# Transposing five mixer tiles by TensorE into PSUM instead of by 32x32 blocks on VectorE, and a wider spread of the in-place norm scaling

## Chip, core and metric

One core of one Trainium2 chip runs the whole layer. The metric is the device time of one execution in microseconds (us). The engines are called by the profile's names: PE is TensorE, with PEld for its weight loads; DVE is VectorE; ACT is ScalarE; POOL is GpSimd; SP is SyncE, which issues the DMAs.

## What is computed

A hybrid decoder layer on 256 positions of width 2048, all in float32, cut here to what matters:

```
x  = LN0(alpha*x + 0.5*SwiGLU_1(x))              # FFN, hidden width 5504
z  = x @ W_in                                    # columns: conv B, C, h | hgrn q, f, i, g | two gates
yA = B * causal_dwconv3(C * h)
f  = lb + (1-lb)*sigmoid(f);  q = silu(q);  k = 1-f
yB = rmsnorm(chunked_gla(q, k, i, log f)) * norm_w * silu(g)
m  = sigmoid(gate_conv)*(yA @ Wa) + sigmoid(gate_hgrn)*(yB @ Wb)
x  = LN1(alpha*x + m @ W_out)
x  = LN2(alpha*x + 0.5*SwiGLU_2(x))
x  = LN3(alpha*x + sigmoid(x @ W_pg) * (p @ W_pp))
```

LN is a layer norm with a gain row and a bias row; layers, batch and depth are 1.

## The kernel before

**Matmuls.** Every product is a list of units. A unit is 512 output columns over up to 16 row blocks of 128, for both halves of the 256 positions (t = 0 and 1, 128 partitions each). Weights come in pairs of row blocks (512 KB, a "weight pair" below): one DMA on SP's queue into a `raw` buffer (4 of them, line 669), one cast by ACT into a high half `wh` (line 682), one subtraction by DVE into a low half `wl` (line 684, the "split"). Six buffers hold such split pairs, a few more in some stages but none more in the mixer. The left operand is held in the same way as high and low halves, so each row block takes three matmuls on PE: high by high (line 736), high by low weight (737), low by high (738), each 128x512, summed in PSUM. Each weight pair serves six of them for t = 0 and six for t = 1. When a unit's sum is complete, its epilogue reads it from PSUM on ACT or DVE.

**Turning tiles.** A result that is to be the left operand of a later product, or that the recurrence needs with channels on partitions, has to be transposed. There are two ways in the code: `transposed` (line 176) has PE multiply four 128x128 pieces with an identity into a PSUM tile `tp` (2 buffers); `turn_blocks` (line 197) has DVE transpose 32x32 blocks, 16 instructions of 32 partitions x 128 elements for a 128x512 tile. The norms use the first way; the FFN's hidden tiles, most of the merge's tiles m and the mixer's f, q, u, b and y use the second. `halves` (line 182) then makes the high half on ACT (line 189) and the low half on DVE (line 190).

**The mixer** runs twice seven units (f, q, i as `v`, g, C as `cst`, h, B as `b`), two groups of four heads each. `hgrn_units` and `conv_units` give the epilogues. `hgrn` is a generator of some 40 steps: kb, qd and AT on DVE, small float32 matmuls on PE (lines 394, 424, 444, 453 to 456), squares and a square root on ACT, then y (line 467).

**Order.** The code counts ticks, one per weight pair and half t, that is every six large matmuls. `defer(n, fn)` runs `fn` n ticks later, and each tick runs one step of the generator. `affine_rows` (line 241) finishes a norm in place: after a norm, x holds only the centred and scaled value; two DMAs of 256 KB on SP's queue bring 512 columns of gain and bias, spread over all partitions, into one of the four `raw` buffers, and four ticks later DVE multiplies and adds for both t (lines 250, 251). This is done for four column groups c after each of the first three norms. `settle(c)` runs deferred work early when the next product needs these columns. On top of this a scheduler in the build orders each engine's instructions by its own timing model; at run time every engine works in that order.

Of the kernel before, what the change touches and what calls it, by code (L numbers as in the profile page):

```python
# [17 lines left out]
P = 128  # L18
# [47 lines left out]
def hybrid_layer(ctx: ExitStack, tc: tile.TileContext, x, p, ln_g, ln_b, ffn1_w_in, ffn1_w_out, mix_w_in,  # L66
# [189 lines left out]
    def layer_norm(t, i, scale, stat):  # L256

        mean, r = moments(t, scale)

        def operand(c, xc):  # L260
            y = st.tile([P, CC], F32, tag="silu", name="y", bufs=2)
            tp = transposed(xc, 4)
            if t == 0 and c < 2:
                gate["pe"] = state["turned"], 1
            for a in range(4):
                k = i * 16 + 4 * c + a
                nc.scalar.activation(y[:, a * P : (a + 1) * P], tp[:, a * P : (a + 1) * P], AF.Identity,  # L267
                                     bias=gbT[:, 48 + k : 49 + k], scale=gbT[:, k : k + 1])
            halves(stat, t, c, y, 4, "x")

        for c in range(4):
            xc = xt[t][:, c * CC : (c + 1) * CC]
            norm = nc.vector.tensor_scalar(out=xc, in0=xc, scalar1=mean, scalar2=r, op0=ALU.subtract, op1=ALU.mult)
            defer((6 if t == 0 else 4) + c, lambda c=c, xc=xc: operand(c, xc))
            if c == 1 and t == 0:
                gate["lo"] = norm.ins, 2
        if t == NT - 1:
            for c in range(4):
                unsettled.add(c)
                defer(16 + 6 * c, lambda c=c: affine_rows(i, c, range(NT)))  # L280

    def layer_norm_out(t, gb):
        mean, r = moments(t, 1.0)
# [100 lines left out]
    def hgrn(j, ys, qT, fT, kT, v, sg):  # L384
# [63 lines left out]
        for t in range(NT):  # L448
            po = ps_h.tile([P, CC], F32, tag="hg", name="po")
            for h in range(4):  # L450
                c = slice(h * P, (h + 1) * P)
                if t == 0:
                    nc.tensor.matmul(po[:, c], AT[:, h, 0, :], v[0][:, c], start=True, stop=True)
                else:
                    nc.tensor.matmul(po[:, c], A01[:, h, :], v[0][:, c], start=True, stop=False)
                    nc.tensor.matmul(po[:, c], AT[:, h, 1, :], v[1][:, c], start=False, stop=True)
            yield
            ss = st.tile([P, 4], F32, tag="ss", name="ss", bufs=2)
            junk = st.tile([P, P], F32, tag="junk", name="junk", bufs=1)
            for h in range(4):  # L460
                nc.scalar.activation(junk, po[:, h * P : (h + 1) * P], AF.Square, accum_out=ss[:, h : h + 1])
            r = rsqrt_of(ss, 4, 1.0 / P, RMS_EPS)
            yield
            y = st.tile([P, CC], F32, tag="h", name="y", bufs=3)
            for h in range(4):
                c = slice(h * P, (h + 1) * P)
                nc.vector.scalar_tensor_tensor(out=y[:, c], in0=po[:, c], scalar=r[:, h : h + 1], in1=sg[t][:, c],
                                               op0=ALU.mult, op1=ALU.mult)
            yield
            yT = rtile([P, 4, P], F32, tag="qd", name="yT", bufs=2)  # L470
            turn_blocks(yT, y, 4)
            halves(ys, t, j, yT.rearrange("p a b -> p (a b)"), 4, "g")
            yield

    ya, yb = Stat(), Stat()
# [1 line left out]
    def hgrn_units(j):  # L477
# [3 lines left out]
        def epi_f(t, acc):  # L481
# [5 lines left out]

            def fn():
                cols = slice(t * P, (t + 1) * P)
                turn_blocks(hold["f"][:, :, cols], s, 4)  # L490
                for h in range(4):
                    i = 4 * j + h
                    nc.vector.tensor_scalar(out=hold["f"][:, h, cols], in0=hold["f"][:, h, cols],
                                            scalar1=oml[:, i : i + 1], scalar2=lb[:, i : i + 1],
                                            op0=ALU.mult, op1=ALU.add)
                nc.vector.tensor_scalar(out=hold["k"][:, :, cols], in0=hold["f"][:, :, cols], scalar1=-1.0, scalar2=1.0,
                                        op0=ALU.mult, op1=ALU.add)

            defer(2, fn)

        def epi_q(t, acc):
            s = st.tile([P, CC], F32, tag="h", name="s", bufs=3)
            nc.scalar.activation(s, acc, AF.Silu)
            defer(2, lambda: turn_blocks(hold["q"][:, :, t * P : (t + 1) * P], s, 4))

        def epi_v(t, acc):
            v[t] = rtile([P, CC], F32, tag=f"v{t}", name="v")
# [13 lines left out]
    def conv_units(j):  # L521
# [6 lines left out]
        def epi_h(t, acc):  # L528
# [6 lines left out]

            def fn():
                uT, cT = hold["u"], hold["c"]
                turn_blocks(uT[:, :, 2 + t * P : 2 + (t + 1) * P], u, 4)
                for h in range(4):
                    i = 4 * j + h  # L540
                    o = cT[:, h, t * P : (t + 1) * P]
# [4 lines left out]
                                                       scalar=cw[:, 8 * kk + i : 8 * kk + i + 1], in1=o,  # L546
                                                       op0=ALU.mult, op1=ALU.add)

            defer(2, fn)

        def epi_b(t, acc):
            b = st.tile([P, CC], F32, tag="h", name="b", bufs=3)
            nc.scalar.copy(b, acc)  # L553

            def fn():
                z = st.tile([P, CC], F32, tag="h", name="z", bufs=3)
                zv = z.rearrange("p (h c) -> p h c", h=4)
                turn_blocks(zv, b, 4)
                nc.vector.tensor_tensor(out=zv, in0=zv, in1=hold["c"][:, :, t * P : (t + 1) * P], op=ALU.mult)
                halves(ya, t, j, z, 4, "g")  # L560

            defer(2, fn)

        for base, epi in ((CW, epi_c), (2 * CW, epi_h), (0, epi_b)):
            units.append(Unit(x1, wm, 0, 16, base + j * CC, CC, epi))
# [210 lines left out]
```

## Time and profile before

| | us |
|---|---|
| median of 3 runs (2276.3 to 2281.53) | 2278.85 |
| the profiled execution, its own time | 2279.4 |
| its span, first to last instruction | 2277.6 |
| PE busy | 2232.2 |
| DVE busy | 1591.9 |
| ACT busy | 996.6 |

The span runs from the first to the last instruction, and 1.8 us of the time lie around it. Stages by time: first FFN to 715, its norm to 745, the mixer's fourteen units to 1088, the merge to 1445, second FFN to 2165, the last product and norm to the end. PE's busy time counts a matmul until its modelled end, so two matmuls 0.23 us apart overlap; the counts of matmuls in a stretch, multiplied by the pace, tell more than the busy share. In the stretches view, PEclk is the granted clock as a share of 2.4 GHz.

### The profile page before, as it was taken

To read this page: it belongs to the slowest core of one execution; us is meant where nothing else is said; L and a number is where in the kernel's file an instruction comes from. 1 tells how busy PE (TensorE), PEld (TensorE's weight loads), DVE (VectorE), ACT (ScalarE), POOL (GpSimd) and SP (SyncE) were. 2 spreads that over 40 slices of the span, in tenths; PEclk is the share of its full clock that TensorE was granted. 3 is DMA by queue.
4 is the path that set the end of the run, shared out by engine and by line. 5 is a ranking of instruction groups with operands and counts; after the bars stand their busy time and mean duration, and the time that the engine had idled before them with its cause. 6 is when DMAs were issued, how large, how long until landed. Compare 5 with 4: busy or idle time off the path is not lost.

```text
span 2277.6 us, 27257 instructions
## 1 busy us (share of the span) xinstructions
PE 2232.2 (98%) x10074; PEld 1856.1 (81%) x10074; DVE 1591.9 (70%) x2534; ACT 996.6 (44%) x1160; POOL 10.5 (0%) x32
## 2 busy tenths in 40 slices
PE   9999999999999999899999999999999999999997
PEld 7888888888897788688788888788888888889875
DVE  6766566755685979978854975678755767467667
ACT  5443444444345343433444444634433444344463
POOL 1000000000000000000000000000000000000000
PEclk9999999999999999999999999999999999999999
DMA  8565566565563564464566565566565666655574
GB/s 284 185 210 196 185 195 198 181 203 192 159 216 118 178 204 137 165 202 128 175 197 199 175 202 194 168 205 231 192 199 184 200 194 197 199 183 185 164 227 148
DMA packets 225337, 430.01 MB, mean 189 GB/s; under 512 B 13740, under 2 KB 22452, under 8 KB 225204
## 3 DMA queue, kind: packets, MB, share of 16 engines
q1 hardware_dynamic: 225204, 428.27, 58.3%
q8 instruction: 79, 1.29, 0.2%
q14 instruction: 54, 0.44, 0.1%
HBM read 426.12 MB, written 2.10 MB: 188 GB/s over the span
## 4 chain that ended last, share of the span: by engine, by line
PE 82%; DVE 11%; DMA 3%; issue 2%; ACT 1%; SPq 0%; DVEq 0%; ACTq 0%
PE acc L737 27%; PE acc L738 27%; PE acc L736 27%; DVE wl L684 3%; DMA gb<-in_ln_g_dram 1%; PE gp L424 1%; DVE yT L202 1%; DVE uT L202 1%; DVE fT L202 1%; DMA raw<-in_ple_w_gate_dram 1%; DMA raw<-in_ffn_w_in_dram 1%; DMA raw<-in_mix_w_in_dram 1%; DVE z L202 1%; ACT y L267 1%; ACT wh L682 0%
## 5 line engine op out<-in xcount | busy, mean ns | idle before, releaser
L682 ACT CAST wh<-raw 128x1024 fp32r<-128x1024 f32 (+2 forms) x804 | 830.7, 1037 | 1063.2 <-PE acc L738 812.6
L684 DVE TENSOR_TENSOR wl<-raw,wh 128x1024 fp32r<-128x1024 f32 (+2 forms) x804 | 958.6, 1207 | 459.1 <-ACT wh L682 425.8
L737 PE MATMUL acc<-wl,xh 128*128 128x512 f32 (+1 forms) x2240 | 869.5, 389 | 11.1 <-DVE wl L684 11.1
L736 PE MATMUL acc<-wh,xh 128*128 128x512 f32 (+1 forms) x2240 | 867.2, 389 | 9.4 <-ACT wh L682 3.8
L738 PE MATMUL acc<-wh,xl 128*128 128x512 f32 (+1 forms) x2240 | 869.8, 389 | 1.8 <-DVE xl L190 1.8
L737 PEld LDWEIGHTS acc<-wl,xh 128*128 128x128 f32 x2240 | 423.0, 189 | 97.5 <-DVE wl L684 15.5
L736 PEld LDWEIGHTS acc<-wh,xh 128*128 128x128 f32 x2240 | 423.0, 189 | 94.5 <-ACT wh L682 5.7
L738 PEld LDWEIGHTS acc<-wh,xl 128*128 128x128 f32 x2240 | 422.9, 189 | 85.6 <-DVE xl L190 3.5
L736 PE MATMUL acc<-wh,gh 128*128 128x512 f32 x880 | 343.1, 390 | 2.9 <-ACT b L553 2.9
L738 PE MATMUL acc<-wh,gl 128*128 128x512 f32 x880 | 342.8, 390 | 0.0
L737 PE MATMUL acc<-wl,gh 128*128 128x512 f32 x880 | 342.5, 389 | 0.0
L202 DVE STREAM_TRANSPOSE hT<-h 32x128 f32<-32x128 f32 (+1 forms) x704 | 210.8, 300 | 9.8
L736 PEld LDWEIGHTS acc<-wh,gh 128*128 128x128 f32 x880 | 165.4, 188 | 37.5 <-ACT b L553 3.4
L738 PEld LDWEIGHTS acc<-wh,gl 128*128 128x128 f32 x880 | 165.3, 188 | 34.1
L737 PEld LDWEIGHTS acc<-wl,gh 128*128 128x128 f32 x880 | 165.3, 188 | 34.0
L309 DVE TENSOR_TENSOR h<-silu,acc 128x512 f32<-128x512 f32 (+1 forms) x44 | 29.6, 672 | 53.1 <-PE acc L738 53.1
L189 ACT CAST gh<-hT 128x512 fp32r<-128x512 f32 (+1 forms) x48 | 29.4, 613 | 63.3 <-DVE hT L202 63.3
L305 ACT ACTIVATE silu<-acc 128x512 f32<-128x512 f32 (+1 forms) x44 | 25.7, 585 | 51.0 <-PE acc L738 51.0
L322 DVE TENSOR_TENSOR x<-x,acc 128x512 f32<-128x512 f32 x32 | 21.8, 683 | 31.2 <-PE acc L738 31.2
L267 ACT ACTIVATE y<-tp,gbT 128x128 f32<-128x128 f32 x96 | 36.2, 474 | 7.9 <-PE tp L179 4.7
L190 DVE TENSOR_TENSOR gl<-hT,gh 128x512 fp32r<-128x512 f32 (+1 forms) x48 | 32.4, 674 | 0.0
L202 DVE STREAM_TRANSPOSE hT<-m 32x128 f32<-32x128 f32 x96 | 29.1, 303 | 1.4
(142 smaller groups left out, 727.0 us busy)
## 6 DMA issues: line engine op xcount, KB each, us to landing
raw<-in_ffn_w_in_dram SPq DMA_DIRECT2D x320, 512.0 KB, 4.7
raw<-in_mix_w_in_dram SPq DMA_DIRECT2D x176, 512.0 KB, 4.7
raw<-in_ffn_w_out_dram SPq DMA_DIRECT2D x168, 512.0 KB, 5.3
raw<-in_mix_w_out_dram SPq DMA_DIRECT2D x32, 512.0 KB, 5.1
raw<-in_ple_w_gate_dram SPq DMA_DIRECT2D x32, 512.0 KB, 5.5
raw<-in_ffn_w_in_dram SPq DMA_DIRECT2D x32, 384.0 KB, 3.9
raw<-in_branch_w_conv_dram SPq DMA_DIRECT2D x16, 512.0 KB, 5.5
raw<-in_branch_w_hgrn_dram SPq DMA_DIRECT2D x16, 512.0 KB, 4.5
```

The costliest lines, as they stand in the source:

```text
L189: nc.scalar.copy(hf, src)
L190: nc.vector.tensor_tensor(out=lf, in0=src, in1=hf.bitcast(F32), op=ALU.subtract)
L202: nc.vector.transpose(dst[32 * b : 32 * b + 32, :nb, 32 * q : 32 * q + 32], cols[32 * q : 32 * q + 32, :, b, :])
L267: nc.scalar.activation(y[:, a * P : (a + 1) * P], tp[:, a * P : (a + 1) * P], AF.Identity, bias=gbT[:, 48 + k : 49 + k], scale=gbT[:, k : ...
L305: nc.scalar.activation(silu[t][:, :w], acc, AF.Silu)
L309: nc.vector.tensor_tensor(out=h[:, :w], in0=silu[t][:, :w], in1=acc, op=ALU.mult)
L424: nc.tensor.matmul(gp[:, (h * 2 + t) * 64 : (h * 2 + t + 1) * 64], kd[:, h, t * P : (t + 1) * P], qd[:, h, t, :], start=True, stop=True)
L682: nc.scalar.copy(h[:, :n, :w], raw[:, :n, :w])
L684: nc.vector.tensor_tensor(out=l[:, :n, :w], in0=raw[:, :n, :w], in1=h[:, :n, :w].bitcast(F32), op=ALU.subtract)
L736: nc.tensor.matmul(acc, sh, wh[:, a, : u.width], start=first, stop=False)
L737: nc.tensor.matmul(acc, sh, wl[:, a, : u.width], start=False, stop=False)
L738: nc.tensor.matmul(acc, sl, wh[:, a, : u.width], start=False, stop=last)
```

## The change

1. The tiles f, q, u, b and y of the mixer are transposed by PE through `transposed` instead of by `turn_blocks` on DVE. f is scaled by DVE straight out of PSUM; q and u are copied from PSUM by ACT; b is multiplied with the convolution's result straight out of PSUM; y goes through `to_stat`, which takes both halves out of PSUM. Where these steps were deferred by 2 ticks they are deferred by 3, and the generator has one more empty step ahead of y's.
2. The four calls of `affine_rows` after each norm are deferred by 40, 60, 80 and 100 ticks instead of 16, 22, 28 and 34.

```diff
-                defer(16 + 6 * c, lambda c=c: affine_rows(i, c, range(NT)))
+                defer(40 + 20 * c, lambda c=c: affine_rows(i, c, range(NT)))
...
             yield
-            yT = rtile([P, 4, P], F32, tag="qd", name="yT", bufs=2)
-            turn_blocks(yT, y, 4)
-            halves(ys, t, j, yT.rearrange("p a b -> p (a b)"), 4, "g")
+            yield
+            to_stat(ys, t, j, y, 4, "g")
...
-                turn_blocks(hold["f"][:, :, cols], s, 4)
+                tp = transposed(s, 4)
                 for h in range(4):
                     i = 4 * j + h
-                    nc.vector.tensor_scalar(out=hold["f"][:, h, cols], in0=hold["f"][:, h, cols],
+                    nc.vector.tensor_scalar(out=hold["f"][:, h, cols], in0=tp[:, h * P : (h + 1) * P],
...
-            defer(2, lambda: turn_blocks(hold["q"][:, :, t * P : (t + 1) * P], s, 4))
+
+            def fn():
+                tp = transposed(s, 4)
+                nc.scalar.copy(hold["q"][:, :, t * P : (t + 1) * P], tp.rearrange("p (h c) -> p h c", h=4))
+
+            defer(3, fn)
...
-                turn_blocks(uT[:, :, 2 + t * P : 2 + (t + 1) * P], u, 4)
+                tp = transposed(u, 4)
+                nc.scalar.copy(uT[:, :, 2 + t * P : 2 + (t + 1) * P], tp.rearrange("p (h c) -> p h c", h=4))
...
+                tp = transposed(b, 4)
                 z = st.tile([P, CC], F32, tag="h", name="z", bufs=3)
                 zv = z.rearrange("p (h c) -> p h c", h=4)
-                turn_blocks(zv, b, 4)
-                nc.vector.tensor_tensor(out=zv, in0=zv, in1=hold["c"][:, :, t * P : (t + 1) * P], op=ALU.mult)
+                nc.vector.tensor_tensor(out=zv, in0=tp.rearrange("p (h c) -> p h c", h=4), in1=hold["c"][:, :, t * P : (t + 1) * P], op=ALU.mult)
                 halves(ya, t, j, z, 4, "g")
```

**DVE, where the first head group's b and y are turned** (z is b turned, then multiplied; yT is y turned; gl the low half of an operand). Before:

```order
L684 TENSOR_TENSOR wl<-raw,wh 128x1024
L202 STREAM_TRANSPOSE z<-b 32x4x32 x11
L202 STREAM_TRANSPOSE yT<-y 32x4x32 x16
L202 STREAM_TRANSPOSE z<-b 32x4x32 x5
L684 TENSOR_TENSOR wl<-raw,wh 128x1024 x4
L559 TENSOR_TENSOR z<-z,cT 128x512
L190 TENSOR_TENSOR gl<-yT,gh 128x512
L202 STREAM_TRANSPOSE z<-b 32x4x32 x13
```

The same place on DVE in the changed kernel, where the split is line 689 and b's product line 564:

```order
L467 SCALAR_TENSOR_TENSOR y<-po,r,sg 128x128 x4
L689 TENSOR_TENSOR wl<-raw,wh 128x1024 x3
L564 TENSOR_TENSOR z<-tp,cT 128x512
L190 TENSOR_TENSOR gl<-tp,gh 128x512
L689 TENSOR_TENSOR wl<-raw,wh 128x1024
L190 TENSOR_TENSOR gl<-z,gh 128x512
L564 TENSOR_TENSOR z<-tp,cT 128x512
L689 TENSOR_TENSOR wl<-raw,wh 128x1024
```

The 32 transposes that stood in one piece between two splits are gone, and between two splits of this piece stand at most two other instructions.

**PE, in the changed kernel, where y of t = 0 is turned** (po is the recurrence's output, suf and AT its operands; lines 741 to 743 are the three large matmuls). In the row of before only the po matmuls stood here:

```order
L743 MATMUL acc<-wh,xl 128x512
L455 MATMUL po<-v,suf 128x128
L179 MATMUL tp<-ident,y 128x128 x2
L456 MATMUL po<-v,AT 128x128
L455 MATMUL po<-v,suf 128x128
L179 MATMUL tp<-ident,y 128x128 x2
L456 MATMUL po<-v,AT 128x128
```

y's transposes now stand in PE's queue among the po matmuls of t = 1, 30 large matmuls behind the po matmuls of t = 0 from which y comes; the large matmuls follow behind them.

**DVE, in the last product, at its third and fourth column group** (sig is the gate, x_92 and x_93 are x of t = 0 and 1, gb the gain and bias). Before:

```order
L250 TENSOR_TENSOR x_92<-x_92,gb 128x512
L250 TENSOR_TENSOR x_93<-x_93,gb 128x512
L684 TENSOR_TENSOR wl<-raw,wh 128x1024
L634 TENSOR_TENSOR sig<-sig,pp 128x512
L251 TENSOR_TENSOR x_92<-x_92,gb 128x512
L251 TENSOR_TENSOR x_93<-x_93,gb 128x512
L635 SCALAR_TENSOR_TENSOR x_93<-x_93,sig 128x512
L215 BN_STATS bn<-x_93 128x6
L684 TENSOR_TENSOR wl<-raw,wh 128x1024 x4
```

The last rows with gain and bias in the changed kernel (lines 639 and 640 are 634 and 635 of before):

```order
L251 TENSOR_TENSOR x_92<-x_92,gb 128x512
L251 TENSOR_TENSOR x_93<-x_93,gb 128x512
L250 TENSOR_TENSOR x_92<-x_92,gb 128x512
L250 TENSOR_TENSOR x_93<-x_93,gb 128x512
L640 SCALAR_TENSOR_TENSOR x_92<-x_92,sig 128x512
L689 TENSOR_TENSOR wl<-raw,wh 128x1024
L640 SCALAR_TENSOR_TENSOR x_93<-x_93,sig 128x512
L251 TENSOR_TENSOR x_92<-x_92,gb 128x512
L251 TENSOR_TENSOR x_93<-x_93,gb 128x512
L215 BN_STATS bn<-x_92 128x6
L215 BN_STATS bn<-x_93 128x6
L639 TENSOR_TENSOR sig<-sig,pp 128x512
```

Before, nine splits follow the last of these scalings; now the last of all splits stands between the multiplication and the addition of the fourth group. On SP's queue the four pairs of loads move behind 789, 795, 803 and 804 of the 804 weight pairs, from 784, 789, 791 and 795; in the mixer they move behind 293, 302, 313 and 322, from 281, 283, 286 and 290.

## Rows read from the trace of the kernel before

**Rows 1.** The page: the span, then busy time, share of the span and instructions of PE and DVE.

```profile
span 2277.6 us, 27257 instructions
PE 2232.2 (98%) x10074; PEld 1856.1 (81%) x10074; DVE 1591.9 (70%) x2534; ACT 996.6 (44%) x1160; POOL 10.5 (0%) x32
```

**Rows 2.** The stretches view: stretch, its length, busy time and count of each engine, granted clock, DMA share, GB/s. First the first FFN, then the mixer, then pieces of the mixer.

```profile
50.00:600.00 550.00, 550.00 (x2428) 455.61 (x2428) 361.05 (x543) 230.22 (x238) 0.00 (x0) 1.00 0.60 194
745.00:1115.00 370.00, 352.31 (x1668) 292.80 (x1668) 322.42 (x646) 147.81 (x187) 3.81 (x3) 0.98 0.53 166
755.00:815.00 60.00, 53.85 (x231) 42.71 (x230) 52.97 (x98) 21.98 (x24) 0.00 (x0) 0.97 0.64 192
815.00:915.00 100.00, 100.00 (x516) 85.36 (x515) 86.37 (x167) 39.77 (x58) 2.77 (x2) 1.00 0.51 160
915.00:960.00 45.00, 37.34 (x148) 29.44 (x147) 43.72 (x102) 16.85 (x19) 0.00 (x0) 0.92 0.44 147
1095.00:1115.00 20.00, 16.12 (x59) 12.43 (x58) 19.36 (x52) 6.87 (x8) 0.00 (x0) 0.83 0.45 148
```

**Rows 3.** The stretches view of line 736 alone (one of the three large matmuls of a row block): PE and PEld busy time and count, granted clock, DMA share, GB/s.

```profile
50.00:600.00 550.00, 314.99 (x809) 151.79 (x810) 1.00 0.60 194
745.00:1115.00 370.00, 176.59 (x449) 86.08 (x449) 0.98 0.53 166
755.00:815.00 60.00, 28.49 (x73) 14.02 (x73) 0.97 0.64 192
815.00:915.00 100.00, 47.85 (x123) 22.94 (x122) 1.00 0.51 160
```

**Rows 4.** The chain of waits, start and us: a group of 16 small matmuls of the recurrence, and four transposes by PE in the merge (tile m). The last row is of the groups view of the merge: those transposes, count, busy us, mean ns of one, idle time before.

```profile
829.17 1.73 PE gp L424 x16
...
1356.39 0.44 PE tp L179 x4
...
L179 PE MATMUL tp<-ident,m 128*128 128x128 f32 x8 | 1.2, 272 | 0.0
```

**Rows 5.** The waits of PE from 745 to 1115 us: who waited for whom, us in all, times, the longest.

```profile
PE acc L737 <- DVE wl L684: 7.8, 7, 3.0
PE acc L736 <- ACT b L553: 5.9, 2, 3.0
PE acc L736 <- ACT wh L682: 3.8, 2, 2.4
```

**Rows 6.** The timeline of DVE around 945 us (start, us, instruction, count).

```profile
938.72 5.04 DVE L202 STREAM_TRANSPOSE fT<-s 32x128 f32<-32x128 f32 x16
943.79 2.36 DVE L684 TENSOR_TENSOR wl<-raw,wh 128x1024 fp32r<-128x1024 f32 x2
...
951.07 1.90 DVE L202 STREAM_TRANSPOSE fT<-s 32x128 f32<-32x128 f32 x6
953.00 3.50 DVE L684 TENSOR_TENSOR wl<-raw,wh 128x1024 fp32r<-128x1024 f32 x3
```

**Rows 7.** The timeline of PE just behind it; in brackets the idle time before an instruction and what ended it.

```profile
954.28 0.54 PE L737 MATMUL acc<-wl,xh 128*128 128x512 f32 x1 [3.02 <-DVE wl L684]
...
955.05 0.63 PE L736 MATMUL acc<-wh,xh 128*128 128x512 f32 x1
955.47 0.63 PE L737 MATMUL acc<-wl,xh 128*128 128x512 f32 x1
```

**Rows 8.** The stretches view of line 202 alone, the transposes on DVE, in the mixer; then the groups view of one of their five tiles (count, busy us, mean ns of one, idle before).

```profile
745.00:1115.00 370.00, 95.58 (x317) 0.98 0.53 166
...
L202 DVE STREAM_TRANSPOSE yT<-y 32x128 f32<-32x128 f32 x64 | 19.4, 303 | 0.8
```

**Rows 9.** The groups view: an ACT copy of 128x512 out of PSUM, the low half made out of PSUM (first products) and out of SBUF (y in the mixer), and ACT's casts of weights in the mixer with their idle time before.

```profile
L446 ACT COPY suf<-gp 128x512 f32<-128x512 f32 x2 | 1.2, 585 | 7.5 <-DVE u L534 7.5
...
L190 DVE TENSOR_TENSOR xl<-tp,xh 128x512 fp32r<-128x512 f32 x8 | 5.4, 687 | 3.6 <-ACT xh L189 3.6
...
L190 DVE TENSOR_TENSOR gl<-yT,gh 128x512 fp32r<-128x512 f32 x4 | 2.7, 686 | 0.0
...
L682 ACT CAST wh<-raw 128x1024 fp32r<-128x1024 f32 x112 | 117.2, 1049 | 178.6 <-PE acc L738 86.8 <-DMA raw<-in_mix_w_in_dram 53.5 <-DVE wl L684 28.6
```

**Rows 10.** The last product: PE's only wait from 2200 to 2264 us; then DVE's timeline: a scaling that waits for its load, the last split, the start of the last norm for t = 0 and for t = 1; then the page of DMAs: the gain's loads, count, size, us from issue to landing.

```profile
PE acc L737 <- DVE wl L684: 2.1, 2, 1.2
...
2229.00 1.29 DVE L250 TENSOR_TENSOR x<-x,gb 128x512 f32<-128x512 f32 x2 [2.62 <-DMA gb<-in_ln_g_dram]
...
2250.20 1.21 DVE L684 TENSOR_TENSOR wl<-raw,wh 128x1024 fp32r<-128x1024 f32 x1
2256.93 0.69 DVE L634 TENSOR_TENSOR sig<-sig,pp 128x512 f32<-128x512 f32 x1 [5.52 <-ACT sig L633]
...
2265.48 0.68 DVE L634 TENSOR_TENSOR sig<-sig,pp 128x512 f32<-128x512 f32 x1
...
gb<-in_ln_g_dram SPq DMA_DIRECT2D x16, 256.0 KB, 5.3
```

**Rows 11.** The timeline of ACT and DVE on the way to y of t = 0: the first square of the recurrence's output, the table load for the square root, y.

```profile
885.76 0.28 ACT L461 ACTIVATE junk<-po 128x128 f32<-128x128 f32 x1 [0.26 <-PE po L453]
...
891.15 1.28 ACT L224 ACT_TABLE_LOAD   x1
...
901.63 1.12 DVE L467 SCALAR_TENSOR_TENSOR y<-po,r,sg 128x128 f32<-128x128 f32 x4
```

More of the change, by code (lines that the diff above doesn't have):

```diff
@@ L497, in fn @@
                                         op0=ALU.mult, op1=ALU.add)
-            defer(2, fn)
+            defer(3, fn)
         def epi_q(t, acc):
@@ L503, in epi_q @@
             nc.scalar.activation(s, acc, AF.Silu)
-            defer(2, lambda: turn_blocks(hold["q"][:, :, t * P : (t + 1) * P], s, 4))
+            def fn():
+                tp = transposed(s, 4)
+                nc.scalar.copy(hold["q"][:, :, t * P : (t + 1) * P], tp.rearrange("p (h c) -> p h c", h=4))
+            defer(3, fn)
         def epi_v(t, acc):
@@ L547, in fn @@
                                                        op0=ALU.mult, op1=ALU.add)
-            defer(2, fn)
+            defer(3, fn)
         def epi_b(t, acc):
@@ L555, in fn @@
             def fn():
+                tp = transposed(b, 4)
                 z = st.tile([P, CC], F32, tag="h", name="z", bufs=3)
                 zv = z.rearrange("p (h c) -> p h c", h=4)
-                turn_blocks(zv, b, 4)
-                nc.vector.tensor_tensor(out=zv, in0=zv, in1=hold["c"][:, :, t * P : (t + 1) * P], op=ALU.mult)
+                nc.vector.tensor_tensor(out=zv, in0=tp.rearrange("p (h c) -> p h c", h=4), in1=hold["c"][:, :, t * P : (t + 1) * P], op=ALU.mult)
                 halves(ya, t, j, z, 4, "g")
-            defer(2, fn)
+            defer(3, fn)
         for base, epi in ((CW, epi_c), (2 * CW, epi_h), (0, epi_b)):
```

## The prediction

> **What bounds the kernel now.** I read the page first, then the stretches, then PE's waits, and last the timelines at each wait. PE is busy for 98% of the span [rows 1], so time can be won only where PE loses some. The stretches show where. In the first FFN PE is busy without a break for 550 us at full clock. Line 736 runs 809 times there, so 3 x 809 = 2427 large matmuls take 550 us, 0.2266 us each [rows 2, 3]. That is the pace of a PE that nothing holds up. The mixer falls behind it: 449 x 3 = 1347 large matmuls make 305.2 us, the other 1668 - 1347 = 321 at 1.73 / 16 = 0.108 us make 34.7 us, and the stretch is 370 us long, so 30 us are lost [rows 2 to 4].
>
> The loss is not spread out. From 815 to 915 us the same sum is 369 x 0.2266 + 147 x 0.108 = 99.5 of 100 us: nothing is lost, though DVE is 86% busy and the whole recurrence of the first group runs there. From 755 to 815 it is 219 x 0.2266 + 12 x 0.108 = 50.9 of 60, so 9.1 us are lost; from 915 to 960, 148 x 0.2266 = 33.5 of 45, 11.5 lost; from 1095 to 1115, 59 x 0.2266 = 13.4 of 20, 6.6 lost [rows 2, 3]. Together these three pieces lose **27.2 us**.
>
> They are the pieces in which f, q, b and y are turned. PE's waits in the mixer name only a split by DVE, a cast by ACT, or the copy of b by ACT that makes room in PSUM [rows 5]. The timeline shows why: 16 transposes hold DVE for 5.04 us, then two splits, then 14 more with what belongs to them, and only at 953.00 the split for which PE has waited 3.02 us [rows 6, 7]. The casts and the copy of b are late for the same reason, since ACT's casts stand behind DVE's splits for 28.6 us of the mixer [rows 9]. After such a wait PE runs at half its clock for a while: the next large matmuls start 0.42 us apart instead of 0.23, and the granted clock of the three pieces is 0.97, 0.92 and 0.83 [rows 2, 7]. The 27.2 us contain both the wait and the slow matmuls behind it.
>
> **The change part by part.** *Transposes off DVE.* The mixer has 317 recorded, 95.6 us at 0.303 us each [rows 8]; the program has 20 tiles x 16 = 320. Without them DVE is busy for 322.4 - 95.6 = 226.8 us of some 350, 65%, the share that it has in the first FFN (361 of 550, 66%), where PE loses nothing [rows 2]. The pieces of 16 and 32 that stand ahead of splits are gone from DVE's order. What is late next is the recurrence's chain and the norm's scaling, and the stretch from 815 to 915 shows that the chain alone costs nothing. I take the whole 27.2 us as won, and as a bound that half of it stays (13.6), should the scaling and the recurrence be enough to hold up a split.
>
> *Transposes onto PE.* 20 tiles x 4 = 80. They are on the path, since PE is the bound. The trace has the same thing in the merge: four of them take 0.44 us of PE's chain between two large matmuls [rows 4]. 20 x 0.44 = **8.8 us** added. At the other end stands the record of one, 0.272 us [rows 4]: if the records did not overlap, 80 x 0.272 = 21.8 us. I take 8.8, since that row is the same instruction with the same neighbours.
>
> *What reads the result.* f's scaling, b's product and y's low half read PSUM instead of SBUF on DVE; the low half takes 0.687 us out of PSUM and 0.686 out of SBUF [rows 9], so I take nothing. q and u cost ACT 8 copies of 0.585 us, 4.7 us [rows 9]. ACT is busy for 148 of 370 us in the mixer [rows 2], and its casts wait for 178.6 us there, half of it for PE to give buffers back [rows 9]; that covers the copies. If the cover failed, 4.7 us would be their cost. The new wait is that ACT and DVE stand still at such a read until PE has come to the transposes; behind it stand casts and splits. In the build's order the transposes of f, q, u and b come 12 to 27 large matmuls, 3 to 6 us, behind the end of their unit, and the splits queued behind them are for weight pairs whose buffers PE gives back only then. I take nothing.
>
> *Deferral by one tick more* moves a step by six large matmuls, 1.4 us; nothing needs these tiles that soon.
>
> *Scaling spread out.* In the mixer and the second FFN the loads and the scaling only move; each is two loads of 256 KB on SP's queue, ahead of a weight pair of 512 KB, and two passes over x per half t on DVE. There the loads then lie about ten weight pairs apart instead of three. In the last product they cannot spread: its units come too soon, so `settle` calls for them early, and each load is issued just before it is needed. A load lands after 5.3 us, and DVE waits 2.62 us at one of these scalings already now; PE loses 2.1 us there [rows 10]. In the changed order the last split stands behind the fourth group's multiplication, and five passes of 0.69 us stand between it and the last norm of t = 0. Before, that split is done at 2251.4 and DVE idles for 5.52 us until the gate comes; t = 1 starts in the very moment in which DVE is free, 2265.48 [rows 10]. So whatever delays DVE by more than the 5.5 us lands on the end. The five passes take 3.4 us; a load ahead of the split makes it wait, 2.6 us by that row. 3.4 + 2.6 - 5.5 = 0.5 us; I take **1 us**, since the loads of the third and the fourth group both have to land ahead of it. Bounds: -2 (PE's present 2.1 us go and the tail is covered) and +4 (the wait is a load's whole 5.3 us, and a little more for the second).
>
> *Sum.* -27.2 + 8.8 + 1 = -17.4 us. The profiled execution took 2279.4 us, so 2262.0; it lies 0.55 above the median of the runs, so the forecast is **2261.5 us**.
>
> **A rule against the change.** What the row shows is above: four transposes in 0.44 us of PE [rows 4]. The Trainium skill, page "VectorE: DVE Perf Modes", section "The three transpose paths", puts a 128x128 transpose at 390 ns on TensorE and 311 ns on VectorE, in bfloat16. By that, 80 x 0.39 = 31.2 us would go onto the bound and the result would be 2284; by the row it is 8.8 and 2261.5. The trace does not agree that a transpose costs PE that much when large matmuls stand on both sides of it. The page "TensorE: Matmul & The Clock Gate", section "Part 4: PE-mode transpose", says that transposes do not count as activity for the clock; in the merge's row the large matmuls behind the four come at 0.23 us again, so here that changes nothing.
>
> **The rivals.**
> *A. The bursts are not what matters.* Half of the loss stays, because the scaling of x (each with its load) and the recurrence still stand ahead of splits. For it: by the order of before, the first norm's scaling falls into the first lost piece. Against it: 815 to 915 us, and the other two pieces, which hold no scaling. 2261.5 + 13.6 = 2275.1.
> *B. PE stands at its own transposes (slower).* PE works in order, so a transpose whose tile is not there yet stops the large matmuls behind it. The place is y of t = 0 and the pair of y of t = 1 and b, in both head groups, four stops. y comes at the end of the longest chain: squares, a table load of 1.28 us, the root, then DVE. Before, it is there 15.9 us after the first square [rows 11], while the order now gives it 30 large matmuls, 6.8 us. Against it: in those 15.9 us DVE did the transposes of u, 10 us by 2 x 5.04, which are gone. A stop like the one from 1095 to 1115 costs 6.6 us with the clock's loss [rows 2]. Between my forecast and no change lie 17.4 us, so it decides from the third stop; with four, 2261.5 + 26.4 = 2287.9.
> *C. Each transpose holds PE for its whole record.* 21.8 instead of 8.8: 2274.5. For it only the record's length; against it the chain's row [rows 4]. The skill's 390 ns, named above, belongs here.
> *D. The end takes it back.* The late scalings cost 4 more and each of the four groups stops PE for 2 us in the last product: 2261.5 + 3 + 8 = 2272.5.
> That the change does not do what it says is excluded by the order: the block transposes of the five tiles are gone and 80 pieces stand on PE.
>
> **How the numbers follow.** Forecast 0.68 (2254 to 2269: the low end is without any cost at the end and with the 2.9 us that the mixer loses outside the three pieces won as well, 2261.5 - 3 - 2.9 = 2255.6, less the spread of the runs; the high end is a quarter of the loss staying). A 0.12, B 0.10, C 0.04, D 0.06. The range is 2254 to 2275: it takes in D, C and most of A, and leaves out B and a part of A. About 0.2%, 4.6 us, is what a measurement of this kernel can tell from no change. Slower by more than that needs B: 0.08. Within it lie a third of A and a mild B: 0.07. Faster: 0.85.
>
> **What would show it.** In the changed profile the mixer should have PE busy without a break as in the first FFN, granted clock 1.00, DVE at about 65%, and be some 18 us shorter; four transposes should take 0.44 us of the chain. B would show as PE waiting at line 179 for DVE or ACT, with the clock falling behind it; A as PE waiting at line 742 for splits; D as DVE waiting for gb behind 2190 us and a later start of the last norm. The forecast is wrong if the lost pieces keep their waits, or if new ones appear at the transposes.

## The result, and the profile after

| | before | after |
|---|---|---|
| median, us | 2277.57 (2275.37 to 2281.53, 4 runs) | 2255.12 (2254.24 to 2255.99, 4 runs) |
| ratio after to before | | 0.9900, interval 0.9882 to 0.9917 |
| profiled execution, its span, us | 2279.4, 2277.6 | 2255.39, 2253.7 |

The change makes the kernel 22.5 us faster; 2261.5 was forecast, and the range of 2254 to 2275 holds the result near its low end. The forecast took the median of 2278.85 as its start; against the 2277.57 measured beside the change, it is -22.5 measured to -17.4 forecast.

Every kernel here runs the same 9600 large matmuls, in an order that differs only in short local exchanges, so both traces can be cut at the same count of large matmuls. The stages, from the start of one's first large matmul to that of the next, in us (differences are taken before rounding; the first matmuls of a stage start before the norm ahead of it is through):

| stage | before | after | difference |
|---|---|---|---|
| start, first FFN | 720.1 | 719.2 | -0.9 |
| the mixer's fourteen units | 367.5 | 355.8 | -11.7 |
| merge | 268.1 | 261.6 | -6.5 |
| m @ W_out | 90.3 | 90.3 | 0 |
| second FFN | 712.1 | 710.8 | -1.2 |
| p @ W_pp, last product, last norm | 119.5 | 115.9 | -3.6 |

The change does not touch the first stage; in the other kernels of the study that leave it alone it takes from 719.1 to 721.4 us, so its 0.9 says nothing.

The page after, in the lines of [rows 1]:

```profile
span 2253.7 us, 27116 instructions
PE 2228.8 (99%) x10154; PEld 1858.6 (82%) x10154; DVE 1498.5 (66%) x2214; ACT 1002.6 (44%) x1168; POOL 9.8 (0%) x32
```

DVE lost 320 instructions and 93 us, PE gained 80 instructions, and PE's share rose. The stretches of [rows 2] and, below the dots, line 741 alone (736 before), as in [rows 3]:

```profile
50.00:600.00 550.00, 550.00 (x2428) 455.59 (x2427) 361.88 (x543) 231.35 (x239) 0.00 (x0) 1.00 0.60 194
745.00:1115.00 370.00, 370.00 (x1831) 311.94 (x1830) 244.82 (x342) 163.38 (x206) 3.11 (x3) 1.00 0.56 179
755.00:815.00 60.00, 60.00 (x270) 49.64 (x269) 34.47 (x34) 29.80 (x33) 0.00 (x0) 1.00 0.60 190
815.00:915.00 100.00, 100.00 (x534) 85.69 (x533) 79.89 (x128) 40.18 (x60) 2.07 (x2) 1.00 0.54 171
915.00:960.00 45.00, 45.00 (x208) 37.19 (x207) 25.75 (x31) 22.42 (x24) 0.00 (x0) 1.00 0.56 183
1095.00:1115.00 20.00, 20.00 (x90) 16.54 (x89) 10.55 (x10) 7.68 (x8) 0.00 (x0) 1.00 0.66 209
...
745.00:1115.00 370.00, 186.15 (x476) 89.23 (x475) 1.00 0.56 179
```

In the three pieces that lost time, DVE falls from 52.97 to 34.47, from 43.72 to 25.75 and from 19.36 to 10.55 us, and PE is busy without a break at granted clock 1.00. The mixer's 370 us hold 476 rows of line 741 instead of 449 of line 736.

Next, PE's waits over the whole span (who waited for whom, us in all, times, the longest), then two groups of transposes in the chain of waits (start, us):

```profile
PE acc L743 <- DVE xl L190: 2.6, 5, 0.8
PE acc L741 <- ACT xh L189: 2.2, 2, 1.4
PE tp L179 <- ACT y L267: 2.1, 3, 0.7
...
PE acc L741 <- ACT pp L630: 0.2, 1, 0.2
```

```profile
749.89 0.44 PE tp L179 x4
...
752.87 0.44 PE tp L179 x4
```

All of the waits of [rows 5] are gone and none took their place: those left belong to the start, the norms and p. Four of the new transposes take 0.44 us of the chain, as in [rows 4].

The timeline of DVE at the end (start, us, instruction, count, idle time before), beside [rows 10]:

```profile
2220.26 1.29 DVE L250 TENSOR_TENSOR x<-x,gb 128x512 f32<-128x512 f32 x2 [1.18 <-DMA gb<-in_ln_g_dram]
...
2226.22 1.22 DVE L689 TENSOR_TENSOR wl<-raw,wh 128x1024 fp32r<-128x1024 f32 x1
...
2232.78 0.69 DVE L639 TENSOR_TENSOR sig<-sig,pp 128x512 f32<-128x512 f32 x1 [2.33 <-ACT sig L638]
```

The late scalings end in time: DVE still idles 2.33 us before the last norm, 5.52 before the change. Even so the end is a little longer: from the start of the last large matmul it takes 14.3 us, 13.6 before the change.

### The profile page after: what moved, and what is told of

Its sections match the earlier page's. It is cut to its first block, busy times and chain, and to the rows that moved or that the text cites. A ratio compares the mean times of both kernels' runs of the same rounds, so it can differ in the third digit from the quotient of the medians.

```text
span 2253.7 us, 27116 instructions
## 1 busy us (share of the span) xinstructions
PE 2228.8 (99%) x10154; PEld 1858.6 (82%) x10154; DVE 1498.5 (66%) x2214; ACT 1002.6 (44%) x1168; POOL 9.8 (0%) x32
## 4 chain that ended last, share of the span: by engine, by line
PE 96%; DVE 2%; DMA 1%; ACT 0%; issue 0%; SPq 0%; DVEq 0%; ACTq 0%
PE acc L741 31%; PE acc L743 31%; PE acc L742 31%; PE gp L424 1%; PE tp L179 1%; DVE wl L689 1%; DMA raw<-in_ple_w_gate_dram 0%; DVE x L273 0%; DVE x L286 0%; DVE x L287 0%; DMA x<-in_x_dram 0%; PE dg L394 0%; ACT y L267 0%; DVE xl L190 0%; ACT L224 0%
## 5 line engine op out<-in xcount | busy, mean ns | idle before, releaser
L250 DVE TENSOR_TENSOR x<-x,gb 128x512 f32<-128x512 f32 x24 | 16.4, 723 | 22.0 <-DMA gb<-in_ln_g_dram 22.0
```

## The experiments

Twelve kernels, each beside the kernel before. "Lost" is, here as in the prediction, a stretch less 0.2266 us for each large matmul and 0.108 for each other one in it.

**1 and 2. Each part alone.** `spread_only` is the kernel before with the second part, `turns_only` the changed kernel without it:

```diff
-                defer(16 + 6 * c, lambda c=c: affine_rows(i, c, range(NT)))
+                defer(40 + 20 * c, lambda c=c: affine_rows(i, c, range(NT)))
```

> The kernel before with the scaling of the norms spread out (40, 60, 80, 100 ticks) and nothing else. Theory (the mixer's loss comes from runs of block transposes ahead of splits): the mixer keeps most of its 27 us, the second FFN wins 1.3 and the last product about 3.5, as between the two traces; 2272 to 2274 us. Rival (the scaling is what holds up the first lost piece): that piece's 9 us go as well, 2264 us.

> The five tiles turned by TensorE, the scaling at 16, 22, 28 and 34 ticks as before. Theory: the three lost pieces of the mixer close, less 8.8 us for the transposes, and the last product keeps its wait for late splits: 2258 to 2261 us. Rival (scaling): 755 to 815 us keeps half of its loss or more, 2264 us or above.

`spread_only`: 2273.06 us, ratio 0.9980 (0.9971 to 0.9988). `turns_only`: 2261.35, ratio 0.9924 (0.9909 to 0.9938). The parts are worth 4 and 16 us alone, 22.5 together. The runs of `turns_only` spread from 2257.6 to 2263.9, and its profiled one is 2.4 us below their median, so its trace shows only 3.4 of the 6.2 us by which it stands behind the changed kernel. The stretches 755 to 815 and 915 to 960 of `spread_only`, then of `turns_only`:

```profile
755.00:815.00 60.00, 56.84 (x246) 45.35 (x245) 48.96 (x90) 25.48 (x27) 0.00 (x0) 1.00 0.63 202
915.00:960.00 45.00, 34.65 (x134) 27.54 (x133) 42.63 (x101) 18.45 (x21) 0.00 (x0) 0.89 0.44 146
```

```profile
755.00:815.00 60.00, 59.85 (x268) 49.09 (x267) 42.69 (x50) 29.17 (x32) 0.00 (x0) 1.00 0.71 216
915.00:960.00 45.00, 45.00 (x208) 37.19 (x207) 25.34 (x31) 22.42 (x24) 0.00 (x0) 1.00 0.57 184
```

Spreading alone halves the loss from 745 to 815 us (9.3 to 4.7): there scaling and turning shared DVE. What the spread takes away there are PE's two waits for a cast (3.8 us, [rows 5]): before each of them ACT waits for a weight load (2.08 us until 776.56, 1.61 until 792.13), and SP issued the first of these right behind a pair of gain and bias loads (768.84 and 769.23, then 769.76). Waits for splits stay, 2.2 us in all before and 3.2 with the spread. The other pieces need the transposes gone. Where `turns_only` stands behind the changed kernel is the second FFN (712.7 against 710.8) and the last product (89.8 against 88.3), by three waits for splits of 2.4 us in all, so this part of the gain belongs to the spread; alone, it has nearly the same 710.7 and 88.2.

**3. The price on PE.** `turns_tripled` lets each of the 20 groups transpose its four pieces three times over.

```diff
-        for i in range(nb):
+        for i in [i for _ in range(times) for i in range(nb)]:
```

> The changed kernel with every transpose of the five tiles made three times into the same PSUM place, 160 more pieces in 20 groups. If a piece costs TensorE 0.108 us between large matmuls, 160 x 0.108 = 17.3 us more than the changed kernel: 2272.5 us. If it holds the engine for its whole record of 0.272 us: 43.5 more, 2298.6 us. If transposes let the clock fall, the granted clock in the mixer falls below 1.00 and it is more than the first sum.

2273.42 us, ratio 0.9979 (0.9970 to 0.9987); the span is 2271.1, 17.4 more than the changed kernel's, for 160 more transposes: 0.109 us each (by the medians 18.3 us, 0.114 each). In the chain twelve take three times what four took:

```profile
750.11 1.31 PE tp L179 x12
```

**4 and 5. Fewer tiles on PE.** `u_on_dve` gives u back to DVE, `uq_on_dve` u and q:

```diff
-                tp = transposed(s, 4)
-                nc.scalar.copy(hold["q"][:, :, t * P : (t + 1) * P], tp.rearrange("p (h c) -> p h c", h=4))
+                turn_blocks(hold["q"][:, :, t * P : (t + 1) * P], s, 4)
```

> The changed kernel with u alone turned by VectorE's blocks again, 64 block transposes of 0.303 us back and 16 pieces on TensorE less. Theory (only runs ahead of a split that is due soon cost): before, nothing was lost where u is turned, so TensorE saves 4 x 0.44 = 1.8 us and nothing waits: 2253.3 us. Rival (every run of 16 costs): 4 runs at about 2 us each, 2261 us.

> The changed kernel with u and q turned by VectorE's blocks again, f, b and y by TensorE. Theory: once f and the scaling are out of the way of q, its runs of 16 alone are hidden as u's are; 2 x 4 x 0.44 = 3.5 us less than the changed kernel, 2251.6 us. Rival: the run of q ahead of a split brings part of the first lost piece back, 2256 us or more.

`u_on_dve`: 2254.07, ratio 0.9894 (0.9878 to 0.9909). `uq_on_dve`: 2252.58, ratio 0.9887 (0.9872 to 0.9902). Its mixer:

```profile
745.00:1115.00 370.00, 369.85 (x1813) 311.18 (x1812) 282.63 (x472) 160.24 (x200) 3.14 (x3) 1.00 0.56 180
```

DVE works 38 us more than in the changed kernel and PE still loses nothing; of the 3.5 us of the 32 transposes that PE is spared, 2.5 show in the median. So block transposes of 5.04 us ahead of splits do not cost as such, with f, b and y out of the way. It is the fastest kernel of the study, though its interval overlaps that of the changed one.

**6. One long piece ahead of each group.** `long_holds` adds 20 DVE instructions to the changed kernel whose result nobody reads, one ahead of each group of transposes:

```diff
+    def hold_dve(src):
+        nc.vector.tensor_reduce(out=keep[0], in_=src.unsqueeze(1).to_broadcast([P, 8, CC]), axis=mybir.AxisListType.X,
+                                op=ALU.max)
```

> The changed kernel with one extra VectorE instruction ahead of each of the 20 groups of transposes: a maximum over 8 x 512 elements a partition that nothing reads, some 4 x 1.2 = 4.8 us by the 128x1024 splits, so about 96 us of VectorE as the block transposes took. Theory (what costs is VectorE held for 5 us ahead of a split that is due): pieces of the mixer lose again, more than 8 us in all, up to the old 27: 2263 to 2282 us. If the loss came from the others waiting for the turned tiles, nothing waits for these and the time stays at 2255.

2255.44 us, ratio 0.9899 (0.9885 to 0.9914): nothing lost. The group of the holds at f and q, and the stretch 915 to 960:

```profile
L205 DVE TENSOR_REDUCE top<-s 128x8 f32<-128x4096 f32 x8 | 35.3, 4415 | 1.4 <-ACT s L511 0.7 <-ACT s L493 0.7
...
915.00:960.00 45.00, 45.00 (x210) 37.23 (x209) 45.00 (x38) 23.44 (x26) 0.00 (x0) 1.00 0.61 193
```

DVE works all 45 of 45 us, in pieces of 4.4 us, and PE runs on. A run of some 5 us ahead of splits is therefore not enough by itself. The other reading that was put down before the run, that the loss came from others waiting for the turned tiles, expects just this time, and this run cannot rule it out; "A second way" below looks at it.

**7. The same work in small pieces.** `turns_scattered` adds three block transposes behind each of 104 splits of the mixer, 312 in all and 93.0 us, read by nobody.

```diff
+        if 272 <= i < 376:
+            spare = rows[0:32, :].rearrange("p (a c) -> p a c", c=32)
+            for q in range(3):
+                cols = h[32 * q : 32 * q + 32, 0, 0:P].bitcast(F32)
+                nc.vector.transpose(spare, cols.rearrange("p (a c) -> p a c", c=32))
```

> The changed kernel with three extra block transposes of a piece of the cast weights, read by nobody, after each of 104 splits of the mixer: 312 x 0.303 = 94.5 us of VectorE, as much as the five tiles took, in pieces of about 0.9 us. Theory (runs): at most 3 us lost, 2255 to 2258 us. Rival (VectorE's share of the time is what costs): the same loss as with long holds.

2261.36 us, ratio 0.9925 (0.9910 to 0.9940): 6 us lost, more than expected. PE's waits in the mixer, and the stretch 815 to 905:

```profile
PE tp L179 <- DVE y L467: 1.2, 3, 0.8
PE acc L747 <- DVE wl L689: 0.8, 1, 0.8
PE gp L424 <- DVE kb L416: 0.5, 1, 0.5
...
815.00:905.00 90.00, 87.24 (x462) 72.53 (x461) 83.96 (x177) 32.17 (x50) 2.00 (x2) 1.00 0.53 157
```

6.3 us are lost from 815 to 905 (1.2 in the changed kernel), where the recurrence runs, and 0.7 from 905 to 965. Delay on DVE reaches PE through kb and y: PE stands at its own small matmuls and at y's transposes. This is rival B's place, and it opens when DVE is loaded again.

**8. Where DVE kept up.** `ffn_by_pe` has PE turn the 44 hidden tiles of the two FFNs too (`to_stat` for `to_stat_blocks`).

> The changed kernel with the 44 hidden tiles of the two FFNs turned by TensorE too, deferred by 3 ticks. Theory: TensorE loses nothing there to VectorE, so the exchange only costs: 40 x 0.44 + 4 x 0.33 = 18.9 us, 2274 us. Rival (less VectorE work always helps): less than 5 us above the changed kernel.

2277.17 us, ratio 0.9993 (0.9983 to 1.0003). The FFNs take 10.9 and 10.2 us more (722.7 from the first large matmul on, and 721.1), 0.123 us for each of the 172 transposes. DVE is relieved of 86 us between 50 and 600 us (361.88 to 275.79), and PE, which lost nothing there, pays for each transpose.

**9 to 11. Length of a piece, or sum over a stretch.** Three kernels of the last four weigh two readings: what counts is the length of one unbroken piece, or the DVE work that piles up over a stretch. `yb_by_pe` leaves f, q and u to DVE. `y_held_twice` is `long_holds` with one hold of 8.7 us at each of y's four tiles alone (16 for 8), `holds_longer` with 6.5 us at all 20 (12 for 8).

> Only b and y are turned by PE; f, q and u go back to block transposes on DVE. 12 tiles fewer on PE, 12 x 0.44 = 5.3 us less PE work than in the changed kernel (2255.1 us): 2249.9 if DVE still has the splits in time. Theory 1 (what cost is that several turned tiles pile up inside some 45 us, more DVE work than there is room beside the splits; y and b at the end of a head group and f at the start of the next): with y and b gone the pile is gone, 2249 to 2251, PE without waits on splits. Theory 2 (f's own two turns, 5.04 us each ahead of splits, cost something by themselves): 2254 to 2260, with waits of PE on splits behind f's turns.

> The changed kernel plus one more DVE instruction ahead of each of y's four tiles, that reads y sixteen times over and takes about 8.8 us in one piece (its result is read by nobody); nothing at the other tiles. 35 us of DVE work more in all, less than the 88 us of the 20 holds of 4.4 us. Theory 1 (what counts is the sum of DVE work over some 45 us against the splits due in it): nothing lost, 2254 to 2257. Theory 3 (what counts is the length of one unbroken piece; 5 us fit into the six split buffers, 8 to 10 us do not): PE waits on splits four times with its slow matmuls behind, 3 us or more each with the clock, 2262 to 2280.

> The changed kernel plus 20 DVE instructions, one ahead of each tile that PE turns, each about 6.6 us long instead of 4.4 (results read by nobody): 132 us more DVE work. In the mixer DVE then has about 226 + 132 = 358 us of work in 350 us, and from 915 to 960 us some 10 us more than it has room for. Theory 1 (sum over a stretch): PE waits on splits in the pieces where holds stand close, the end of the first head group above all, 8 to 25 us lost, 2263 to 2280. Theory 3 (only unbroken pieces of 8 us or more cost): nothing or little lost, 2254 to 2258.

`yb_by_pe`: 2255.41, ratio 0.9902 (0.9887 to 0.9917), 5 above the 2250 expected. The stretches 755 to 815 and 915 to 960, and PE's waits in the mixer:

```profile
755.00:815.00 60.00, 56.54 (x244) 45.21 (x243) 48.70 (x90) 25.58 (x27) 0.00 (x0) 1.00 0.63 202
...
915.00:960.00 45.00, 45.00 (x198) 36.80 (x197) 39.86 (x92) 21.84 (x23) 0.00 (x0) 1.00 0.52 171
...
PE acc L740 <- DVE wl L687: 3.5, 5, 1.1
```

At the end of the first head group, where b, y and f had met, f alone costs nothing. The 5 us are lost from 745 to 815, behind f's and q's first turns. The time lies in the range of theory 2, the place at 915 to 960 speaks for theory 1; each is half right.

`y_held_twice`: 2260.18, ratio 0.9925 (0.9910 to 0.9940), 5 lost, below the 2262 to 2280 of the theory of length and above the 2257 of the other. DVE's timeline at the hold that cost something, and PE's row behind it:

```profile
911.96 8.68 DVE L205 TENSOR_REDUCE both<-y 128x16 f32<-128x8192 f32 x1
920.55 3.49 DVE L697 TENSOR_TENSOR wl<-raw,wh 128x1024 fp32r<-128x1024 f32 x3
...
921.82 0.80 PE L750 MATMUL acc<-wl,xh 128*128 128x512 f32 x1 [2.63 <-DVE wl L697]
```

Only this one of the four holds stops PE. Between it and the hold before it DVE had also scaled x in four passes; the other three holds, as long, cost next to nothing. `holds_longer`: 2270.9, ratio 0.9970 (0.9959 to 0.9981), 15.8 lost, within the 8 to 25 of the theory of the sum. The places are not the ones that it named: from 905 to 965, the end of the first head group, 3.0 us are lost, from 745 to 815 5.4, from 965 to 1050 4.7, and from 1115 to 1140 4.3. There PE waits 2.0 us for ACT's cast of z, b's product, which stands behind a hold on DVE: not a split is late, but the operand. The stretches 755 to 815 and 1095 to 1115 of `holds_longer`, and PE's waits in the mixer:

```profile
755.00:815.00 60.00, 57.17 (x264) 47.17 (x263) 57.53 (x50) 24.80 (x27) 4.21 (x1) 0.97 0.57 178
...
1095.00:1115.00 20.00, 18.88 (x91) 15.28 (x89) 19.17 (x23) 13.96 (x23) 0.00 (x0) 1.00 0.55 177
...
PE acc L754 <- DVE wl L701: 4.6, 3, 2.3
```

**12. The same work, moved.** `b_later` is `spread_only` with b's turns of the first head group put off into the second:

```diff
-            b = st.tile([P, CC], F32, tag="h", name="b", bufs=3)
+            b = st.tile([P, CC], F32, tag="h" if j else "silu", name="b", bufs=3 if j else 2)
...
-            defer(2, fn)
+            defer(2 if j else 48 + 10 * t, fn)
```

> No transposes by PE at all: the kernel before with the scaling spread out (2273.1 us by itself) and one more edit: in the first head group b's two block transposes and its product are deferred by 48 and 58 ticks instead of 2, into the units of the second group that ask little of DVE; b waits in the tile that the C result has left. The same DVE work, moved away from y's and f's turns. In the second head group nothing is moved. From 915 to 960 us the spread kernel loses 45 - 134 x 0.2266 = 14.6 us, from 1095 to 1115 some 20 - 58 x 0.2266 = 6.9 us. Theory 1 (what costs is the sum of DVE work over some 45 us against the splits due in it): with 10 to 12 us of DVE work gone from that stretch most of the 14.6 us comes back, 2259 to 2265, and the loss at 1095 to 1115 stays. Theory 2 (the turns of y and f cost by themselves, wherever b's are): 2269 to 2274, with PE waiting for splits behind y's and f's turns as before.

2269.83 us, ratio 0.9963 (0.9949 to 0.9977): 3 below `spread_only`, not the 8 to 14 of the first theory, and inside the range of the second (2269 to 2274). The stretch 915 to 960, PE's waits in the mixer, then DVE's timeline and PE's longest wait:

```profile
915.00:960.00 45.00, 39.72 (x167) 32.16 (x166) 40.73 (x91) 20.68 (x22) 0.00 (x0) 0.96 0.53 172
...
PE acc L737 <- DVE wl L684: 12.6, 12, 4.4
PE acc L736 <- ACT b L553: 3.0, 1, 3.0
```

```profile
928.17 5.06 DVE L202 STREAM_TRANSPOSE fT<-s 32x128 f32<-32x128 f32 x16 [0.69 <-ACT s L486]
933.26 2.36 DVE L684 TENSOR_TENSOR wl<-raw,wh 128x1024 fp32r<-128x1024 f32 x2
935.54 1.11 DVE L493 TENSOR_SCALAR fT<-fT,oml,lb 128x128 f32<-128x128 f32 x4
936.57 4.08 DVE L202 STREAM_TRANSPOSE fT<-s 32x128 f32<-32x128 f32 x13
...
943.36 0.78 PE L737 MATMUL acc<-wl,xh 128*128 128x512 f32 x1 [4.43 <-DVE wl L684]
```

From 905 to 965 the loss falls from 15.4 to 8.3, and 3.3 of it come back from 965 to 1050 (0.7 to 4.0), where b's turns now stand beside q's. Behind y's turns f's bring only two splits in 14 us, in which PE uses five. The edit also did something that the expectation did not name: the wait of 3.2 us for the copy of b, which `spread_only` has in this stretch, is gone, so the 7.1 us are not all the pile's.

**The pile, counted.** A weight pair lasts PE 12 x 0.2266 = 2.72 us, and six buffers of split pairs 16.3. Go through DVE's timeline of the mixer, add the time of every instruction, and at each split take off 2.72 us and 0.108 for each small matmul among the twelve large ones ahead of that pair's, never below zero. What stands there is by how much DVE's work has run ahead of PE's; PE's standstill is not taken off. The highest value in two stretches, and what PE lost in them:

| kernel | 905 to 965: pile, lost | 1050 to 1115: pile, lost |
|---|---|---|
| `spread_only` | 30.5, 15.4 | 23.4, 7.6 |
| before | 28.0, 11.7 | 23.4, 7.4 |
| `b_later` | 19.5, 8.3 | 23.9, 7.5 |
| `holds_longer` | 17.9, 3.0 | 16.5, 1.6 |
| `y_held_twice` | 14.9, 4.9 | 14.7, 0.6 |
| `turns_scattered` | 14.4, 0.7 | 10.8, 0.5 |
| `long_holds` | 13.3, 0.3 | 13.5, 0.5 |
| `yb_by_pe` | 8.9, 0.8 | 11.8, 0.4 |
| `uq_on_dve` | 8.4, 0.3 | 11.9, 0.4 |
| after | 3.9, 0.3 | 6.1, 0.2 |

In these stretches at most 0.8 us is lost up to 14.7, and 1.6 or more from 14.9 on, not far from the 16.3 us that the buffers hold. No finer border can be read from it: with the small matmuls among the pair's own twelve taken off instead, entries move by up to 2.1 us, `long_holds` to 14.7 and 15.3, and `y_held_twice` to 16.7 and 16.8, of which one lost 4.9 us and the other 0.6. This account was made after the runs; no run was made to test it. Behind a loss it reads too high: from 965 to 1050 the kernel before still has 27.5 with 0.7 lost. At the mixer's start it does not hold: `yb_by_pe` loses 5.0 us from 745 to 815 with a pile of 9.1, `long_holds` 0.1 with 9.5. Why stays open.

**A second way, beside the splits.** In the kernel before, the first wait of PE in the stretch 915 to 960 is not for a split. The timelines of DVE, ACT and PE at the end of the first head group:

```profile
916.45 5.05 DVE L202 STREAM_TRANSPOSE yT<-y 32x128 f32<-32x128 f32 x16
...
921.54 0.62 ACT L189 CAST gh<-yT 128x512 fp32r<-128x512 f32 x1 [3.12 <-DVE yT L202]
922.06 0.58 ACT L553 COPY b<-acc 128x512 f32<-128x512 f32 x1
...
922.69 0.49 PE L736 MATMUL acc<-wh,xh 128*128 128x512 f32 x1 [2.97 <-ACT b L553]
924.42 0.79 PE L737 MATMUL acc<-wl,xh 128*128 128x512 f32 x1 [1.24 <-DVE wl L684]
```

ACT stands 3.12 us until DVE has turned y; the copy of b, which makes room in PSUM, is next on ACT, and PE waits 2.97 us for it. The second head group shows the same at 1103.86 to 1105.01 us, 2.99 and 2.94 us. These are the 5.9 us in the second line of [rows 5], of 17.5 in all, so the turned tile itself held up PE too, through ACT. In `b_later` the first group's copy runs at 905.82, ahead of y's cast, and this wait is gone there; in the changed kernel the cast reads what PE has turned, and the wait is gone in both groups. The holds cannot show this way at y's tiles, since nothing there reads what they make. In the table, what before and `spread_only` lost in both stretches, and `b_later` in the second, contains such a wait, 2.9 to 3.2 us each, with the slow matmuls behind it. No run parts the two ways.

## Why the prediction was right, point by point

- **Where the time is lost: right.** The three pieces give their time back and nothing else in the mixer does. Mixer and merge are 18.2 us shorter; -27.2 + 8.8 = -18.4 was predicted.
- **Why it is lost: right in the engine, too narrow in the mechanism.** Two steps do not hold. "The pieces of 16 and 32 that stand ahead of splits" do not cost by themselves: holds of 4.4 us and the turns of u and q cost nothing (experiments 5, 6). The runs show a loss at the ends of the head groups where turns of three tiles, with products and low halves, met within 45 us; that this sum against the stock of split pairs decides is an account that fits two stretches, is not tested, and fails at the mixer's start. And the copy of b is not late "for the same reason" as the splits: ACT stands for y being turned, and this is 5.9 of the 17.5 us for which PE waits in the mixer.
- **PE's price, 8.8 us: right.** 0.109 us a piece (experiment 3). The Trainium skill's 390 ns in bfloat16 ("VectorE: DVE Perf Modes", "The three transpose paths"), by which an estimate would have been 31.2 us, does not hold among large matmuls here.
- **ACT's copies, reading out of PSUM, the tick more: right at nothing.** No wait names them.
- **The last product, +1: wrong, and so is its bound.** Of the -3.6 in the last row of the table of stages, the last product has -3.0, the end +0.7 and p @ W_pp -1.3. The first two make -2.3, just below the -2 that was the low end. The term counted PE's wait of 2.1 us as the most to be won; the product also held slow matmuls behind that wait, 0.9 of its 3.0 us. The cost at the end is near its size, but not for its reason: DVE waits 1.18 us for its load, not 2.6, and idles 2.33 before the last norm. Instead the gate of t = 0 is ready only 6.7 us ahead of the last large matmul, 7.1 before the change, so DVE is busy with t = 0 for longer and begins t = 1 0.9 us after its gate is ready (2241.33 after 2240.45), 0.4 before the change; the rest of the 0.7 lies behind that. In p @ W_pp two waits of PE for p's operand (1.3 us) fell to 0.2; the other kernels take from 13.1 to 14.9 us there, whether DVE or PE turns the tiles, so this 1.3 cannot be put down to the change.
- **The second FFN, 0: wrong by 1.2.** One wait of 0.91 us for a split, at 1521.6 us behind two passes each of multiplying and adding and 16 block transposes, was overlooked in the trace of before.
- **The number.** Between the two traces lie 23.9 us, 6.5 more than the 17.4 forecast: 1 + 3.6 = 4.6 from the last row, 1.2 from the second FFN and 0.9 from the first stage, less 0.2 in mixer and merge. That the range of 2254 to 2275 holds 2255.1 is partly luck: its low end was reckoned with the 2.9 us that the mixer loses outside the three pieces won as well, and some 3 us are still lost there; what carried the time so low were terms that the sum put at 0 and +1, and scatter.
- **Rivals.** A: no loss stays; but without the spread only 0.7 is lost from 745 to 815, and without the turns moved 4.7, so scaling and turns shared that piece. B: PE waits at none of the mixer's transposes; with DVE loaded it does (experiment 7). C: excluded by experiment 3. D: of the wrong sign.

## What to carry to other kernels

Moving work from an engine at 70% to one at 98% pays where the full engine waits for the other in known places, and only there: the same exchange won 18 us in the mixer and cost 21 in the FFNs. Before moving a burst, add up the helper's work between the pieces that the bound engine consumes and compare it with what the buffers between them hold: that count is a first guess, not a rule that these runs prove, but an average share, or the longest single piece, told less. Look also at what a third engine has queued behind its wait for the burst, as the copy of b here. Then move only the tiles that stand where the loss is: giving two of the five back cost nothing.

## What was not expected of the hardware

- Twelve transposes in a row take PE 1.31 us and four take 0.44, so among large matmuls they run at 0.109 us each although a record is 0.272 us long; the granted clock of the mixer stays 1.00 with 80 of them.
- The length of PE's last wait does not tell whether the granted clock falls. In `yb_by_pe` five waits of up to 1.1 us leave 755 to 815 at 1.00, and in `y_held_twice` one of 2.63 us brings 915 to 960 to 0.96 and costs 4.9 us in all. But in `holds_longer` a wait of 2.33 us, until 767.65, is followed by 1.00, and the clock falls only at 797, with no longer wait than 0.51 us (until 782.54) in between:

```profile
765.00:797.00 32.00, 29.17 (x146) 24.09 (x144) 30.70 (x25) 12.46 (x14) 1.08 (x1) 1.00 0.48 152
797.00:801.00 4.00, 4.00 (x15) 3.29 (x14) 4.00 (x5) 1.04 (x1) 3.13 (x1) 0.57 0.94 306
```
